# Eleven load buffers, an earlier second load, shared fills and straight programs in a fused matmul, mask and softmax

## The chip, the cores and the metric

One core of one Trainium2 chip. The metric is device time in microseconds (us) of one execution, lower is better. A kernel was run several times; a "profile" is one execution with the hardware profiler on. On one core, an execution is labelled slow when it took over 1.5% more than the fastest of the same kernel in the same set of runs.

## The reference

```
batch, m, k, n = 16, 512, 512, 512        # all float32
y = scale * (x @ weight)                  # scale = 0.125
y = where(mask == 1, y, -1e9)             # mask: strictly below the diagonal
out = softmax(y, axis=-1)
```

x is 16.8 MB, weight 1 MB, the result 16.8 MB.

## The kernel before

The work is cut into 16 units: four batches times a quarter (128) of the rows, 1 MB in, 1 MB out. A unit with quarter q needs only (q + 1) x 128 columns, the rest of its output is zero and is filled once in each output buffer. Per unit: VectorE casts x to bf16, TensorE transposes it, VectorE and ScalarE each move half of the transposes out of PSUM, TensorE multiplies with W and adds the mask on the diagonal block by one more matmul, ScalarE takes the exponential with its row sums, VectorE normalises. SyncE issues every transfer, in this order:

```python
BUFS = 8
load(0)
nc.sync.dma_start(w_f32, weight...)
load_mask(3)
load(1); load(2); load(3); load_mask(2); load(4); load_mask(1)
load(5); load_mask(0); load(6); load(7)
nc.sync.wait_ge(s_fill, 1)
for u in range(U):                                  # U = 16
    b = u % BUFS
    nc.sync.wait_ge(s_norm, u + 1)                  # unit u is normalised
    nc.sync.dma_start(out_r[...], ots[b]...)        # store u
    if u + BUFS < U:
        load(u + BUFS)                              # only now: the ninth load follows the first store
```

TensorE's start (cut):

```python
spin(WARM)                        # 12 idle matmuls, to have the clock up (1.0 from 6.3 us on in the first profile)
transpose(0, k)
spin(8)
tensor.wait_ge(s_spread, 1)
tensor.wait_ge(s_wbf, 2)          # both halves of W are cast
for j in range(1, Q):
    transpose(j, k)               # unit 1 is transposed ...
    multiply(j - 1, k)            # ... ahead of the product of unit 0
```

VectorE and ScalarE run loops of two passes over the eight buffers, with branches at their ends. GpSimd fills six parts of output buffers and prepares the mask.

The softmax here doesn't subtract the row's maximum and nothing guards it: scores larger than these inputs give would overflow.

## Time and profile before

| | first profile of the kernel before |
|---|---|
| timed runs | 94.63 us median (94.43 to 94.68) |
| the profiled execution itself | 93.16 us, span 91.0 us |
| traffic | 34.90 MB, mean 384 GB/s |
| busiest compute engine | PE 67% of the span |
| time from issue to landing, loads / stores | 14.0 / 12.3 us (medians) |

The lines themselves stand in the prediction. To read them: a row of slices gives the busy share of 40 equal parts of the span in tenths; GB/s is what the 16 DMA engines moved in each; a stretch's line ends in granted TensorE clock, DMA share and GB/s; a timeline line starts with start and duration in us.

### The profile page before, as it was taken

What the parts mean: (1) busy time and instruction counts of PE and PEld (TensorE: products, weight loads), DVE (VectorE), ACT (ScalarE), POOL (GpSimd) and SP (SyncE); (2) the same over time, 40 slices, a digit from 0 to 9 for tenths busy, and PEclk for the clock granted to TensorE, in tenths of its full rate; (3) what the DMA queues carried; (4) which work ended last, traced back from release to release, by engine and by line L of the source; (5) the groups of instructions that cost most, each with busy time, mean ns of one, the idle gap of its engine ahead of it and who ended that gap; (6) DMA issues with size and microseconds to landing.
All of it is one profiled execution on the core that took longest, in us unless ns stands there. A gap on an engine that the chain in (4) does not pass through costs nothing.

```text
span 91.0 us, 1718 instructions
## 1 busy us (share of the span) xinstructions
PE 60.8 (67%) x592; PEld 42.4 (47%) x596; DVE 56.6 (62%) x70; ACT 52.9 (58%) x149; POOL 11.1 (12%) x18
## 2 busy tenths in 40 slices
PE   0894904999986699998399999817999594000000
PEld 0333404466865547697364778806465483000000
DVE  1005555809999992999997499969281999600000
ACT  0700941778978468897978889734788495000000
POOL 3770596101700000000000000000000000000000
PEclk9999999999999999999999999999999999655555
DMA  0999999999999999999999999999999999999940
GB/s 7 328 396 384 412 418 405 398 375 424 426 421 328 263 378 418 429 425 407 443 411 439 414 421 439 407 439 414 425 436 411 443 414 439 421 421 432 418 202 11
DMA packets 5331, 34.90 MB, mean 384 GB/s; under 512 B 592, under 2 KB 1104, under 8 KB 1104
## 3 DMA queue, kind: packets, MB, share of 16 engines
q1 hardware_dynamic: 5328, 34.87, 94.3%
q8 instruction: 1, 0.02, 0.1%
q14 instruction: 2, 0.02, 0.1%
HBM read 18.09 MB, written 16.78 MB: 383 GB/s over the span
## 4 chain that ended last, share of the span: by engine, by line
DMA 31%; DVE 29%; PE 12%; issue 9%; SPq 4%; DVEq 0%
DMA xf<-in_x_dram 31%; DVE xb L214 13%; DVE ot L227 10%; PE py L332 7%; DVE xt L218 5%; PE pt L317 4%; SPq L123 2%; DVE rinv L225 1%; SPq L119 1%; SPq L142 1%; SPq L126 1%; PE py L339 0%; DVE ot L233 0%; DVEq L213 0%; DVEq L224 0%
## 5 line engine op out<-in xcount | busy, mean ns | idle before, releaser
L332 PE MATMUL py<-w_bf,xt 128*128 128x384 bf16 (+3 forms) x252 | 39.2, 298 | 0.2
L298 ACT ACTIVATE ot<-py 128x512 f32<-128x512 f32 (+3 forms) x64 | 27.8, 439 | 6.0 <-PE py L339 4.4
L214 DVE CAST xb<-xf 128x2048 bf16<-128x2048 f32 x16 | 20.6, 1288 | 11.4 <-DMA xf<-in_x_dram 11.4
L317 PE MATMUL pt<-ident_bf,xb 128*128 128x128 bf16 x256 | 17.2, 220 | 12.4 <-DVE xb L214 12.3
L332 PEld LDWEIGHTS py<-w_bf,xt 128*128 128x128 bf16 x256 | 21.0, 98 | 8.7 <-issue 0.2
L274 ACT COPY xt<-pt 128x1024 bf16<-128x1024 bf16 x16 | 16.2, 1010 | 15.3 <-PE pt L317 15.3
L227 DVE TENSOR_TENSOR ot<-ot,rinv 128x2048 f32<-128x2048 f32 (+3 forms) x16 | 23.9, 1492 | 0.5
L317 PEld LDWEIGHTS pt<-ident_bf,xb 128*128 128x128 bf16 x256 | 15.0, 114 | 15.7 <-DVE xb L214 15.2
L218 DVE COPY xt<-pt 128x1024 bf16<-128x1024 bf16 x16 | 11.0, 686 | 8.4 <-PE pt L317 8.3
L339 PE MATMUL py<-diag_bf,spread 128*128 128x128 bf16 x64 | 14.0, 219 | 0.0
L298 ACT ACTIVATION_READ_ACCUMULATOR ot<-py 128x1 f32 x64 | 12.7, 199 | 0.0
L352 PE MATMUL idle<-zeros 128*128 128x512 bf16 x20 | 6.5, 488 | 2.6 <-DVE zeros L238 2.6
L339 PEld LDWEIGHTS py<-diag_bf,spread 128*128 128x128 bf16 x64 | 6.3, 98 | 3.1
L162 POOL MEMSET ot<- 128x512 f32 (+2 forms) x6 | 6.0, 1008 | 1.5 <-issue 1.1
L352 PEld LDWEIGHTS idle<-zeros 128*128 128x128 bf16 x20 | 2.3, 119 | 5.8 <-issue 5.0
L187 POOL TENSOR_SCALAR diag_bf<-diag_f 128x128 bf16<-128x128 f32 x4 | 2.5, 634 | 11.3 <-DMA diag_f<-in_mask_dram 11.3
L225 DVE RECIPROCAL rinv<-rsum 128x4 f32<-128x4 f32 x16 | 2.7, 170 | 0.0
L274 ACT ACT_TABLE_LOAD x2 | 2.6, 1283 | 0.0
L280 ACT ACT_TABLE_LOAD x1 | 1.3, 1283 | 2.2 <-issue 2.2
L165 POOL MEMSET ot<- 4x384 f32 x2 | 1.8, 890 | 0.1
L238 DVE MEMSET zeros<- 128x256 uint32 x1 | 0.3, 272 | 1.6 <-SPq L64 1.6
L286 ACT CAST w_bf<-w_f 128x1024 bf16<-128x1024 f32 x1 | 1.0, 1049 | 0.0
(9 smaller groups left out, 2.9 us busy)
## 6 DMA issues: line engine op xcount, KB each, us to landing
xf<-in_x_dram SPq DMA_DIRECT2D x16, 1024.0 KB, 14.0
out_dram<-ot SPq DMA_DIRECT2D x16, 1024.0 KB, 12.3
w_f<-in_weight_dram SPq DMA_DIRECT2D x1, 1024.0 KB, 7.9
diag_f<-in_mask_dram SPq DMA_DIRECT2D x4, 64.0 KB, 12.2
```

The costliest lines, as they stand in the source:

```text
L162: pool_step(nc.gpsimd.memset(ots[b][:, :, NC:], 0.0))
L187: nc.gpsimd.tensor_scalar(out=diag_bf[:, q], in0=diag_f32[:, q], scalar1=-MASK_NEG, scalar2=MASK_NEG, op0=ALU.mult, op1=ALU.add,)
L214: vector.tensor_copy(xb, xfs[u % BUFS]).then_inc(s_cast[u % Q], 1)
L218: vector.tensor_copy(xts[u % 2][:, 2:4], pts[1]).then_inc(s_evv[u % Q], 1)
L225: vector.reciprocal(rinvs[b], rsums[b]).then_inc(s_inv[b], 1)
L227: mul = vector.tensor_tensor(out=ot, in0=ot, in1=rinvs[b].unsqueeze(2).to_broadcast([P, T, NC]), op=ALU.mult)
L274: scalar.copy(xts[u % 2][:, 0:2], pts[0]).then_inc(s_eva[u % Q], 1)
L298: scalar.activation(out=ots[j][:, t, :NC], in_=pys[t][:, :NC], func=AF.Exp, bias=0.0, scale=float(scale), accum_out=rsums[j][:, t : t + 1] ...
L317: last = tensor.transpose(pts[kt // 2][:, kt % 2, t], xb[:, t].rearrange("p (k kt) -> p kt k", kt=KT)[:, kt], ident_bf,)
L332: tensor.matmul(pys[t][:, :NC], lhsT=xts[j % 2][:, kt, t], rhs=w_bf[:, kt, :NC], start=(kt == 0), stop=(kt == KT - 1),)
L339: tensor.matmul(pys[t][:, q * P : NC], lhsT=spread[:, t], rhs=diag_bf[:, q], start=False, stop=True, skip_group_check=True,).then_inc(s_py ...
L352: tensor.matmul(idle, lhsT=zeros[:, :P], rhs=zeros, start=True, stop=True)
```

## The change

Its intent: let the transfers never wait for compute. Three more loads are issued before the first store; the second load goes ahead of W, so that TensorE can transpose unit 1 while W arrives; fills leave GpSimd in part; loops become straight programs.

```diff
-BUFS = 8
+X_BUFS = 11
+OUT_BUFS = 8
 ...
     load(0)
+    load(1)
     nc.sync.dma_start(w_f32, weight...)
     load_mask(3)
-    load(1)
     load(2)
-    load(3) ... load(7)                         # with the masks between
-    nc.sync.wait_ge(s_fill, 1)
+    for u in range(3, X_BUFS):
+        load(u)
+        if u < Q + 2:
+            load_mask(Q + 1 - u)
+    nc.sync.wait_ge(s_fill, 3)
 ...
-        if u + BUFS < U:
-            load(u + BUFS)
+        if u + X_BUFS < U:
+            load(u + X_BUFS)
 ...  # VectorE: for u in range(U), no loop registers; W is cast after unit 1's cast and eviction
 ...  # ScalarE: three fills ahead of its first eviction; unit 1 is evicted ahead of W's cast
 ...  # TensorE:
                 spin(8)
-                tensor.wait_ge(s_spread, 1)
-                tensor.wait_ge(s_wbf, 2)
 ...
                     transpose(j, k)
+                    if j == 1:
+                        with tensor.If(k < 2):
+                            spin(4)
+                            tensor.wait_ge(s_spread, 1)
+                            tensor.wait_ge(s_wbf, 2)
                     multiply(j - 1, k)
```

More of the change, by code (lines that the diff above doesn't have):

```diff
@@ L57 @@
     U = B
-    PASSES = U // BUFS
     x_r = x.rearrange("(c e) (q p t) k -> c q p e (t k)", e=E, q=Q, t=T)
@@ L87 @@
     zeros = sbuf("zeros", [P, N], BF16)
-    ots = [sbuf(f"ot{i}", [P, T, N], FP32) for i in range(BUFS)]
-    xfs = [sbuf(f"xf{i}", [P, T, K], FP32) for i in range(BUFS)]
+    ots = [sbuf(f"ot{i}", [P, T, N], FP32) for i in range(OUT_BUFS)]
+    xfs = [sbuf(f"xf{i}", [P, T, K], FP32) for i in range(X_BUFS)]
     xb = sbuf("xb", [P, T, K], BF16)
     xts = [sbuf(f"xt{i}", [P, KT, T, P], BF16) for i in range(2)]
-    rsums = [sbuf(f"rsum{i}", [P, T], FP32) for i in range(BUFS)]
-    rinvs = [sbuf(f"rinv{i}", [P, T], FP32) for i in range(BUFS)]
+    rsums = [sbuf(f"rsum{i}", [P, T], FP32) for i in range(OUT_BUFS)]
+    rinvs = [sbuf(f"rinv{i}", [P, T], FP32) for i in range(OUT_BUFS)]
     pts = [psum(f"pt{i}", [P, 2, T, P], BF16) for i in range(2)]
@@ L98 @@
     s_issued = sem("s_issued")
-    s_x = sem("s_x", BUFS)
-    s_o = sem("s_o", BUFS)
+    s_x = sem("s_x", X_BUFS)
+    s_o = sem("s_o", OUT_BUFS)
     s_mask = sem("s_mask", Q)
@@ L108, with nth, right @@
     s_exp = sem("s_exp", Q, T)
-    s_inv, s_mul = sem("s_inv", BUFS), sem("s_mul", BUFS)
-    s_norm = sem("s_norm")
+    s_own, s_norm = sem("s_own"), sem("s_norm")
     def quarter(u):
         return Q - 1 - u % Q
+    def nth(u):
+        return u // Q + 1
+    def right(b):
+        return ots[b][:, :, (quarter(b) + 1) * P :]
     def load(u):
-        b = u % BUFS
+        b = u % X_BUFS
         nc.sync.dma_start(xfs[b].rearrange("p t k -> p (t k)"), x_r[u // Q, quarter(u)]).then_inc(s_x[b], 16)
@@ L125 @@
     load(0)
+    load(1)
     nc.sync.dma_start(w_f32, weight.rearrange("(p kt) n -> p kt n", kt=KT)).then_inc(s_w, 16)
     load_mask(3)
-    load(1)
     load(2)
-    load(3)
-    load_mask(2)
-    load(4)
-    load_mask(1)
-    load(5)
-    load_mask(0)
-    load(6)
-    load(7)
-    nc.sync.wait_ge(s_fill, 1)
+    for u in range(3, X_BUFS):
[3 more added lines that the diff above has]
+    nc.sync.wait_ge(s_fill, 3)
     for u in range(U):
-        b = u % BUFS
+        b = u % OUT_BUFS
         nc.sync.wait_ge(s_norm, u + 1)
         nc.sync.dma_start(out_r[u // Q, quarter(u)], ots[b].rearrange("p t n -> p (t n)")).then_inc(
-            s_o[b] if u + BUFS < U else s_end, 16
+            s_o[b] if u + OUT_BUFS < U else s_end, 16
         )
-        if u + BUFS < U:
-            load(u + BUFS)
+        if u + X_BUFS < U:
+            load(u + X_BUFS)
     nc.sync.sem_inc(s_issued, 1)
@@ L157, in pool_step @@
         nc.gpsimd.wait_ge(s_pool, steps)
-    def fill(b):
-        NC = (quarter(b) + 1) * P
-        if NC < N:
-            pool_step(nc.gpsimd.memset(ots[b][:, :, NC:], 0.0))
-        if NC == P:
-            pool_step(nc.gpsimd.memset(ots[b][0:E, 0, NC:], 1.0 / N))
     pool_step(nc.gpsimd.memset(ident_bf, 0.0))
@@ L178 @@
         nc.gpsimd.sem_inc(s, 1)
-    for s in s_o:
-        nc.gpsimd.sem_inc(s, 16)
-    for b in range(BUFS // 2):
-        fill(b)
+    for b in range(1, Q):
+        pool_step(nc.gpsimd.memset(right(b), 0.0))
+    nc.gpsimd.sem_inc(s_fill, 1)
+    nc.gpsimd.wait_ge(s_fill, 2)
+    for b in range(Q - 1, OUT_BUFS, Q):
+        pool_step(nc.gpsimd.memset(right(b)[0:E, 0], 1.0 / N))
+    nc.gpsimd.sem_inc(s_fill, 1)
     for j in range(Q):
@@ L185 @@
         nc.gpsimd.wait_ge(s_mask[q], 16)
-        pool_step(
-            nc.gpsimd.tensor_scalar(
-                out=diag_bf[:, q],
-                in0=diag_f32[:, q],
-                scalar1=-MASK_NEG,
-                scalar2=MASK_NEG,
-                op0=ALU.mult,
-                op1=ALU.add,
-            )
-        )
-        nc.gpsimd.sem_inc(s_diag, 1)
-        if j == 0:
-            for b in range(BUFS // 2, BUFS):
-                fill(b)
-            nc.gpsimd.sem_inc(s_fill, 1)
+        nc.gpsimd.tensor_scalar(
+            out=diag_bf[:, q],
+            in0=diag_f32[:, q],
+            scalar1=-MASK_NEG,
+            scalar2=MASK_NEG,
+            op0=ALU.mult,
+            op1=ALU.add,
+        ).then_inc(s_diag, 1)
     nc.gpsimd.wait_ge(s_issued, 1)
@@ L209, with cast, evict_v, normalise @@
     vector = nc.vector
-    def cast(u, k, m):
-        vector.wait_ge(s_x[u % BUFS], m * 16)
-        vector.tensor_copy(xb, xfs[u % BUFS]).then_inc(s_cast[u % Q], 1)
-    def evict_v(u, k):
-        vector.wait_ge(s_ptb[u % Q], k)
+    def cast(u):
+        b = u % X_BUFS
+        vector.wait_ge(s_x[b], 16 * (u // X_BUFS + 1))
+        vector.tensor_copy(xb, xfs[b]).then_inc(s_cast[u % Q], 1)
+    def evict_v(u):
+        vector.wait_ge(s_ptb[u % Q], nth(u))
         vector.tensor_copy(xts[u % 2][:, 2:4], pts[1]).then_inc(s_evv[u % Q], 1)
-    def normalise(u, k, m):
-        b, j = u % BUFS, u % Q
+    def normalise(u):
+        b, j = u % OUT_BUFS, u % Q
         NC = (quarter(u) + 1) * P
         ot = ots[b][:, :, :NC]
-        vector.wait_ge(s_exp[j][T - 1], k + 1 if j >= Q - 2 else k)
-        vector.reciprocal(rinvs[b], rsums[b]).then_inc(s_inv[b], 1)
-        vector.wait_ge(s_inv[b], m)
+        vector.wait_ge(s_exp[j][T - 1], nth(u) + (j >= Q - 2))
+        vector.reciprocal(rinvs[b], rsums[b]).then_inc(s_own, 1)
+        vector.wait_ge(s_own, 2 * u + 1)
         mul = vector.tensor_tensor(
@@ L230, in normalise @@
         if NC == P:
-            mul.then_inc(s_mul[b], 1)
-            vector.wait_ge(s_mul[b], m)
+            mul.then_inc(s_own, 1)
+            vector.wait_ge(s_own, 2 * u + 2)
             vector.memset(ots[b][0:E, 0, :NC], 1.0 / N).then_inc(s_norm, 1)
@@ L235, in normalise @@
             mul.then_inc(s_norm, 1)
+            vector.sem_inc(s_own, 1)
     vector.addr_align(LINE, max_nops=0)
-    vector.memset(zeros, 0.0).then_inc(s_zero, 1)
-    cast(0, 1, 1)
-    evict_v(0, 1)
-    vector.wait_ge(s_w, 16)
-    vector.tensor_copy(w_bf[:, 0:2], w_f32[:, 0:2]).then_inc(s_wbf, 1)
-    cast(1, 1, 1)
-    evict_v(1, 1)
-    cast(2, 1, 1)
-    with vector.Fori(1, PASSES + 1) as m:
-        ks = [m * 2 + (i - 1) for i in range(3)]
-        ks.append(None)
-        for j in range(BUFS):
-            def ahead():
-                evict_v(j + 2, ks[(j + 2) // Q])
-                if j + 3 < BUFS:
-                    cast(j + 3, None, m)
-            def far():
-                if j + 2 >= BUFS:
-                    evict_v(j + 2, ks[(j + 2) // Q])
-                cast(j + 3, None, m + 1)
-            if j + 2 < BUFS:
-                ahead()
-            if j + 3 >= BUFS:
-                with vector.If(m < PASSES):
-                    far()
-            normalise(j, ks[j // Q], m)
+    with vector.Fori(0, 2) as n, vector.If(n > 0):
+        vector.memset(zeros, 0.0).then_inc(s_zero, 1)
+        cast(0)
+        evict_v(0)
+        cast(1)
+        evict_v(1)
+        vector.wait_ge(s_w, 16)
+        vector.tensor_copy(w_bf[:, 0:2], w_f32[:, 0:2]).then_inc(s_wbf, 1)
+        cast(2)
+        for u in range(U):
+            if u + 2 < U:
+                evict_v(u + 2)
+            if u + 3 < U:
+                cast(u + 3)
+            normalise(u)
@@ L270, with evict_s @@
     scalar = nc.scalar
-    def evict_s(u, k):
-        scalar.wait_ge(s_pta[u % Q], k)
+    def evict_s(u):
+        scalar.wait_ge(s_pta[u % Q], nth(u))
         scalar.copy(xts[u % 2][:, 0:2], pts[0]).then_inc(s_eva[u % Q], 1)
     scalar.addr_align(LINE, max_nops=0)
-    with scalar.Fori(0, 2) as n, scalar.If(n > 0), scalar.Fori(1, PASSES + 1) as m:
-        with scalar.If(m < 2):
-            scalar.wait_ge(s_ident, 1)
-            scalar.copy(
-                spread.rearrange("k t (p e) -> k t p e", e=E),
-                ident_bf.rearrange("k (p t) -> k t p", t=T).unsqueeze(3).to_broadcast([P, T, P // T, E]),
-            ).then_inc(s_spread, 1)
-            evict_s(0, 1)
-            scalar.wait_ge(s_w, 16)
-            scalar.copy(w_bf[:, 2:4], w_f32[:, 2:4]).then_inc(s_wbf, 1)
-        ks = [m * 2 + (i - 1) for i in range(3)]
-        for j in range(BUFS):
-            if j + 1 < BUFS:
-                evict_s(j + 1, ks[(j + 1) // Q])
-            else:
-                with scalar.If(m < PASSES):
-                    evict_s(j + 1, ks[(j + 1) // Q])
-            NC = (quarter(j) + 1) * P
-            scalar.wait_ge(s_o[j], m * 16)
+    with scalar.Fori(0, 2) as n, scalar.If(n > 0):
+        scalar.wait_ge(s_ident, 1)
+        scalar.copy(
+            spread.rearrange("k t (p e) -> k t p e", e=E),
+            ident_bf.rearrange("k (p t) -> k t p", t=T).unsqueeze(3).to_broadcast([P, T, P // T, E]),
+        ).then_inc(s_spread, 1)
+        scalar.wait_ge(s_zero, 1)
+        for b in range(Q + 1, OUT_BUFS):
+            NF = N - (quarter(b) + 1) * P
+            fill = scalar.copy(right(b), zeros[:, :NF].unsqueeze(1).to_broadcast([P, T, NF]))
+        fill.then_inc(s_fill, 1)
+        evict_s(0)
+        evict_s(1)
+        scalar.wait_ge(s_w, 16)
+        scalar.copy(w_bf[:, 2:4], w_f32[:, 2:4]).then_inc(s_wbf, 1)
+        for u in range(U):
+            b, j = u % OUT_BUFS, u % Q
+            NC = (quarter(u) + 1) * P
+            if 0 < u < U - 1:
+                evict_s(u + 1)
+            if u >= OUT_BUFS:
+                scalar.wait_ge(s_o[b], 16 * (u // OUT_BUFS))
@@ L296 @@
             for t in range(T):
-                scalar.wait_ge(s_py[j % Q][t], ks[j // Q])
+                scalar.wait_ge(s_py[j][t], nth(u))
                 scalar.activation(
-                    out=ots[j][:, t, :NC],
+                    out=ots[b][:, t, :NC],
                     in_=pys[t][:, :NC],
@@ L303 @@
                     scale=float(scale),
-                    accum_out=rsums[j][:, t : t + 1],
-                ).then_inc(s_exp[j % Q][t], 1)
+                    accum_out=rsums[b][:, t : t + 1],
+                ).then_inc(s_exp[j][t], 1)
     tensor = nc.tensor
@@ L376 @@
     with tc.tile_critical(no_gpsimd_drain=True):
-        nc.sync.wait_ge(s_end, 16 * BUFS)
+        nc.sync.wait_ge(s_end, 16 * OUT_BUFS)
         nc.sync.sem_clear(s_end)
```

## The prediction

> **What bounds the kernel now.** I read the page's slices first, because they show whether one resource is busy from end to end.
>
> ```profile
> DVE  1005555809999992999997499969281999600000
> ACT  0700941778978468897978889734788495000000
> DMA  0999999999999999999999999999999999999940
> GB/s 7 328 396 384 412 418 405 398 375 424 426 421 328 263 378 418 429 425 407 443 411 439 414 421 439 407 439 414 425 436 411 443 414 439 421 421 432 418 202 11
> ```
>
> A slice is 2.275 us. The DMA row is at 9 from the second slice to the second-last but one; no compute row is, and all of them are empty in the last 5 to 6 slices while transfers go on. So the 16 DMA engines bound the kernel: 34.90 MB in a span of 91.0 us. The rate has three defects: a start (328 to 384), a dip to 263 around slice 13, and a tail. I put numbers on them with busy time by stretch (us, busy times of the engines, granted clock, DMA share, GB/s last).
>
> ```profile
> 10.00:20.00 10.00, 6.30 (x51) 3.62 (x51) 4.97 (x5) 5.74 (x11) 5.14 (x6) 1.00 1.01 401
> 20.00:28.00 8.00, 7.62 (x91) 6.19 (x89) 7.37 (x8) 7.04 (x21) 1.93 (x2) 1.00 1.01 422
> 28.00:33.00 5.00, 3.54 (x41) 2.47 (x39) 4.97 (x7) 3.02 (x12) 0.00 (x0) 1.00 0.99 283
> 34.00:80.00 46.00, 36.18 (x384) 26.85 (x383) 36.41 (x48) 33.56 (x103) 0.00 (x0) 0.98 1.01 425
> 80.00:85.00 5.00, 0.00 (x0) 0.00 (x0) 0.00 (x0) 0.00 (x0) 0.00 (x0) 0.50 1.03 434
> ```
>
> Steady traffic of loads and stores mixed runs at 425, stores alone at 434, loads alone at 422 once the mask loads are through. The dip, 28 to 33 us, moves 283. It costs 5 x (1 - 283/425) = 1.67 us. Its DMA share is 0.99: the engines were **not empty** in it. The packet records of the trace say the same: an 8 KB packet takes 309 ns nearly everywhere, but in these 5 us many take 400 to 660 ns and five take 1.3 to 1.95 us.
>
> What the dip coincides with is in the timeline of the queue that issues:
>
> ```profile
> 24.89 0.61 SPq L142 DMA_DIRECT2D out_dram<-ot  x1
> 25.54 0.60 SPq L119 DMA_DIRECT2D xf<-in_x_dram  x1
> 28.44 0.60 SPq L142 DMA_DIRECT2D out_dram<-ot  x1
> 29.08 0.84 SPq L119 DMA_DIRECT2D xf<-in_x_dram  x1
> 31.52 0.60 SPq L142 DMA_DIRECT2D out_dram<-ot  x1
> 32.16 1.03 SPq L119 DMA_DIRECT2D xf<-in_x_dram  x1
> ```
>
> The first store is issued at 24.89 and the ninth load at 25.54, when the eight first loads are still draining (the eighth was issued by 10.6 and lands 17.2 us after its issue, near 27.2). So the dip begins just as the engines pass from loads to the first store, with two transfers queued and the next pair coming at 28.44. That makes two readings possible: a **thin queue**, or a **first store that is slow by itself**. This is the fork of the whole prediction.
>
> Last, the chain that ended last:
>
> ```profile
> 4.37 8.09 DMA xf<-in_x_dram
> 12.47 0.02 issue
> 12.49 2.33 DVE xb L214
> 14.82 0.05 issue
> 14.87 1.08 PE pt L317 x16
> 15.95 0.05 issue
> 16.00 0.81 PE py L332 x3
> ```
>
> Compute of the first unit (4 batches x 128 rows; there are 16) begins only at 16.00, since TensorE transposes unit 1 ahead of the first product, unit 1 lands at 12.47 behind W, and its cast takes 2.33 us. This start is late, but it is on the path that sets the end only in so far as it delays transfers.
>
> [...] the store issued at 24.89 lands 5.9 us later (30.8), after the eighth load. So in the changed kernel the first store stands behind eleven loads. [...] the cast that ran from 12.49 beside a GpSimd fill took 2.32 us, the median of that row is 1217 ns. [...] the register steps on VectorE's sequencer in the chain are 0.04 to 0.05 us each.
>
> **The change part by part.**
>
> *Second load ahead of W.* Each MB takes about 2.6 us at the early rate of 401. The first load lands at 7.1 (0.96 + 6.1) as before; the second now near 9.7 in place of 12.47; W near 12.2 in place of 9.6. The cast of unit 1 can end near 10.9, its transposes near 12.1, and then W is the last to come: 12.2 + 1.05 (ScalarE's cast of its half) = 13.25. The first product starts near 13.3 in place of 16.0: 2.7 us earlier. The first store, 8.9 us after it (24.89 - 16.00), comes near 22.2. No byte of traffic is removed, and the transfers of these first 13 us are merely permuted: 0 us at the end by itself.
>
> *Fills shared.* Three memsets of GpSimd (3.31 us from 10.43) become three copies on ScalarE. As estimates they cost about as much (512, 1024 and 1536 elements a row, some 3.5 us), from 4 to 7.6 us, ahead of the first eviction at 9.1: hidden. The cast loses its 1.1 us of blocking. Off the DMA path: 0 us.
>
> *Straight programs.* Register steps and branches go: some 0.05 to 0.2 us a unit on VectorE. Where VectorE is the pace, four stores come in 15.33 us (40.16 to 55.49), 3.83 a unit, against 2 MB a unit at 425, 4.9 us. VectorE is not the pace of the transfers: 0 us.
>
> *Eleven load buffers.* Before the first store there are now 11 loads, W and the masks: 11 x 1.049 + 1.049 + 0.26 = 12.85 MB. At 402 GB/s, from 2.4 us, that lasts to about 34.3. By then (first store 22.2, then about 3 to 4 us each, as before) four stores and four loads are queued. The queue is never thin: 8 MB in place of 2. The last load moves up, from 70.35 to about 60. After it there are only stores; the DMA engines reach store k (from the sixth on) at 59 + 2.45 (k - 5), hence the last at 83.5, and compute has it ready by about 77 (3.83 x 15 + 22.2 less the uneven last unit), so no gap opens there. Output buffers stay at eight: the thirteenth unit's exponential (near 60) needs the fifth store (near 58); close, but with slack of 4 us at the end.
>
> *Sum.* Transfers after the change: 2.4 + 12.85 MB/402 + 22.0 MB/425 = 2.4 + 32.0 + 51.8 = 86.2, plus the tail. The same sum for before, 9.7 MB/402 + 25.2 MB/425 = 24.1 + 59.3, plus 2.4 and the 1.67 of the dip, gives 87.5. The tail and the end are equal. The longer stretch of loads at 402 is an artefact of the masks in it, which do not grow; with 422 for the three added loads the difference is the dip alone, **1.67 us if it goes altogether, 0 if it stays**.
>
> **The rivals.** *A: thin queue.* With 8 MB queued the dip goes: 94.63 - 1.67 = 93.0; since the five engines that were held for 1 to 1.6 us longer may be those that finish last (the slice rates fall 418, 202, 11), perhaps up to 1 us more: 92.0. For it: the dip sits exactly where the queue is thinnest, and the rate is full from 34 on, with the queue deeper. Against it: the first store and ninth load were queued over 2 us before their turn and the share is 0.99. *B: the first stores are slow whenever they come,* [...]. Then the dip moves to 34 us and the time stays at 94.3 to 94.6. For it: the slow packets are those of the first store itself. Against it: stores alone at 80 to 85 us run at 434. *C: compute or the eight output buffers become the bound* after the loads have run ahead: stores late, a new gap near 60 to 75 us, 95 or more. For it: the fifth store comes close to the exponential that needs it; against it: 4 to 6 us of slack for the last stores.
>
> **Range and chances.** I give A a little over half[...], and B a little under half: 0.53 x 92.7 + 0.44 x 94.4 + 0.03 x 95.5 = 93.5. The runs of before spread by 0.25 us. Two per cent faster means below 92.74, which needs the whole dip and some of the tail: about 0.25. Over 2% slower needs C at its worst: 0.02. The range that should hold it 8 times in 10 is 92.0 to 94.7.
>
> **What would show it.** First product near 13.3 and first store issued near 22: the compute part. Rate in 28 to 33 at 420 and no dip near 34 to 39: A. A dip of the same depth, moved to about 34 to 39, with DMA share near 1: B. Last load landing near 60. Waits of ScalarE for a store, or a DMA share below 0.9 between 55 and 80: C. The prediction is wrong if the start of the transfers itself moves, or if the engines that finish last are not relieved although the dip goes.

## The result

The changed kernel took **91.14 us** (median, 91.02 to 91.44, 4 runs), the kernel before 94.66 us (94.43 to 96.43, 4 runs). The ratio of the fast runs is 0.9641, 95% interval 0.9607 to 0.9674; a ratio here is the mean time of one kernel's fast runs over that of the other's in the same rounds, so not quite the ratio of the medians. The kernel is 3.6% faster. The prediction said 93.5, with 92.0 to 94.7: too little gain, and the time lies outside of the range.

The profile of the changed kernel (91.09 us, span 89.3) answers to the lines above. First the slices:

```profile
DVE  0105545329999983999997499999669994000000
ACT  0199444688977478897558889746798960000000
DMA  0999999999999999999999999999999999999940
GB/s 7 305 404 407 417 409 421 368 380 415 424 418 429 433 426 418 426 422 429 415 426 426 422 426 429 426 418 433 426 422 426 426 429 418 429 433 426 426 187 11
```

The dip of the thirteenth and fourteenth slices is gone and none has come elsewhere: from the tenth slice to the 38th the rate stays between 415 and 433. By stretch, same columns as before:

```profile
28.00:33.00 5.00, 3.77 (x32) 2.36 (x33) 4.93 (x8) 2.73 (x8) 0.00 (x0) 1.00 1.01 426
...
40.00:80.00 40.00, 28.77 (x315) 21.57 (x312) 30.87 (x41) 25.60 (x86) 0.00 (x0) 0.97 1.01 426
80.00:85.00 5.00, 0.00 (x0) 0.00 (x0) 0.00 (x0) 0.00 (x0) 0.00 (x0) 0.50 1.02 429
```

283 became 426 where the dip was; the steady stretch stayed what it was (425, now 426), and stores alone ran at 429 for 434. The queue that issues:

```profile
23.91 0.61 SPq L145 DMA_DIRECT2D out_dram<-ot  x1
24.57 0.60 SPq L126 DMA_DIRECT2D xf<-in_x_dram  x1
27.46 0.60 SPq L145 DMA_DIRECT2D out_dram<-ot  x1
28.10 0.60 SPq L126 DMA_DIRECT2D xf<-in_x_dram  x1
```

The first store is issued only 1 us earlier than before, but its turn on the DMA engines comes near 34 (33.95) instead of 27 (26.54), behind eleven loads. Last, the chain at the start:

```profile
10.52 1.14 DVE xb L206
11.66 0.05 issue
11.71 0.65 PE pt L299 x8
12.36 0.02 issue
12.38 1.01 ACT xt L253
13.39 0.95 ACT w_bf L270
14.35 0.47 issue
14.82 1.02 PE py L314 x4
```

The first product starts at 14.82 instead of 16.00; ScalarE first evicts unit 1 (1.01) and then casts W, which I had not put in the sum.

So at this point the mechanism looks like my rival A. What does not fit is the size: the spans of the two profiles differ by 1.7 us, which is the dip, and the times by 3.5.

### The profile page after: what moved, and what is told of

The parts are those of the page before. It is cut to its first block, busy times and chain, and to the rows that moved or that the text cites. A ratio compares the mean times of both kernels' runs of the same rounds, so it can differ in the third digit from the quotient of the medians.

```text
span 89.3 us, 1698 instructions
## 1 busy us (share of the span) xinstructions
PE 61.1 (68%) x599; PEld 42.7 (48%) x600; DVE 55.3 (62%) x70; ACT 52.7 (59%) x150; POOL 5.9 (7%) x15
## 4 chain that ended last, share of the span: by engine, by line
DVE 27%; PE 26%; issue 20%; DMA 7%; ACT 2%; SPq 0%; DVEq 0%
PE py L314 16%; DVE xb L206 15%; PE pt L299 10%; DVE xt L210 9%; DMA xf<-in_x_dram 7%; DVE rinv L217 1%; ACT xt L253 1%; DVE ot L219 1%; ACT w_bf L270 1%; PE py L321 1%; DVE ot L225 0%; DVEq L231 0%; SPq L397 0%; SPq L64 0%
## 5 line engine op out<-in xcount | busy, mean ns | idle before, releaser
L314 PE MATMUL py<-w_bf,xt 128*128 128x512 bf16 (+3 forms) x256 | 40.0, 299 | 1.2 <-ACT w_bf L270 1.2
L206 DVE CAST xb<-xf 128x2048 bf16<-128x2048 f32 x16 | 19.5, 1218 | 5.8 <-DMA xf<-in_x_dram 5.8
L265 ACT CAST ot<-zeros 128x512 f32<-128x512 bf16 (+2 forms) x3 | 2.9, 1040 | 0.0
L175 POOL MEMSET ot<- 128x512 f32 (+2 forms) x3 | 2.9, 951 | 0.6 <-issue 0.5
L185 POOL TENSOR_SCALAR diag_bf<-diag_f 128x128 bf16<-128x128 f32 x4 | 1.5, 375 | 12.6 <-DMA diag_f<-in_mask_dram 12.6
L180 POOL MEMSET ot<- 4x384 f32 x2 | 0.8, 408 | 3.9 <-ACT ot L265 3.9
```

Of the source, the lines that this page charges most:

```text
L175: pool_step(nc.gpsimd.memset(right(b), 0.0))
L206: vector.tensor_copy(xb, xfs[b]).then_inc(s_cast[u % Q], 1)
L265: fill = scalar.copy(right(b), zeros[:, :NF].unsqueeze(1).to_broadcast([P, T, NF]))
L314: tensor.matmul(pys[t][:, :NC], lhsT=xts[j % 2][:, kt, t], rhs=w_bf[:, kt, :NC], start=(kt == 0), stop=(kt == KT - 1),)
```

## The experiments

Five sets of two to four kernels, each set on one chip together with runs of the kernel before. Since the label "fast" in a set depends on how lucky the fastest run of the kernel before was (92.23 in the first set), most verdicts against it read "unclear"; I give medians and ranges of all runs. Each set ran on another chip, and the median of the kernel before lies between 94.31 and 95.19 in them, so a difference between two sets is rougher than one within a set.

**1. The kernel before once more** (no edit).

> The kernel before, unchanged, run as if it were the change, so that every run's span is listed and another execution is profiled. Theory 1 (my base was a lucky execution): the profiled execution that I predicted from took 93.16 us with a span of 91.0, 1.5 us less than the timed runs (94.63); then the runs here should have spans of about 92.5 and a profile whose dip between 28 and 33 us, or whose tail, costs some 1.5 us more than in the first one. Rival (the gain lies outside the span, in the launch): spans stay near 91.0 while the times are 94.6. Ratio to before 1.00.

Measured: 94.79 us (91.65 to 95.54, 4 runs) and 95.19 (92.23 to 96.46, 7 runs) for the same kernel. The kernel before is not one number: it spreads by 4 us, while the changed one spreads by 0.4. Of its 45 recorded executions four took 91.65 to 92.71 us, less than my first profile; none of them was profiled, so what made them fast stays open. The profiled execution took 95.54 with a span of 93.4, so the missing time is inside the span, as theory 1 says.

**2. Straight programs alone**: the kernel before with VectorE and ScalarE unrolled as in the change.

```diff
-    with vector.Fori(1, PASSES + 1) as m: ...
+    for u in range(U):
+        if u + 2 < U: evict_v(u + 2)
+        if u + 3 < U: cast(u + 3)
+        normalise(u)
```

> The kernel before with one part of the change alone: straight programs on VectorE and ScalarE; eight load buffers, W first, GpSimd fills. If straight programs carry nothing: ratio 1.00 to before, and the same mixture of fast and slow executions (92 to 96). Rival (branches and register steps were on the path of the first stores): first store about 0.5 us or more earlier and 1% less time.

Measured: 95.65 us (95.25 to 97.08) beside 94.76 (93.64 to 95.61) for the kernel before; ratio 1.0135 (1.0009 to 1.026). Straight programs by themselves bring nothing; if anything they lose 1.4%, which no run explains (the recorded verdict is unclear). Their profile (95.77 us) shows where the kernel with eight buffers and W first loses more than in my first profile. TensorE at the start, the idle time before an instruction in brackets:

```profile
10.73 1.24 PE L336 MATMUL idle<-zeros 128*128 128x512 bf16 x5
15.62 1.08 PE L301 MATMUL pt<-ident_bf,xb 128*128 128x128 bf16 x16 [3.64 <-DVE xb L217]
```

and the stretches of the same execution (granted clock, DMA share, GB/s last):

```profile
15.00:20.00 5.00, 4.32 (x26) 2.30 (x28) 2.38 (x3) 1.70 (x3) 1.21 (x2) 0.67 1.02 419
26.00:28.00 2.00, 2.00 (x28) 1.86 (x27) 2.00 (x3) 2.00 (x7) 0.00 (x0) 1.00 0.50 209
28.00:33.00 5.00, 3.21 (x50) 2.78 (x49) 4.93 (x7) 3.17 (x15) 0.00 (x0) 1.00 0.91 315
33.00:40.00 7.00, 6.95 (x61) 4.42 (x61) 5.28 (x8) 5.51 (x13) 0.00 (x0) 1.00 1.00 364
```

While it waits for unit 1 behind W, TensorE stands still for 3.64 us. After that its granted clock is 0.5 for 3.41 us (16.73 to 20.14 in the trace's clock records), a mean of 0.67 over this stretch. The first products come slower (four matmuls of 128x512 take 1.91 us instead of 1.03), the first store is issued at 27.32 instead of 24.89 (0.75 of these 2.4 us were lost before the clock fell, since unit 1's transposes start at 15.62 instead of 14.87), and now the queue does run out: DMA share 0.50 between 26 and 28. At 425 GB/s the lost time is 2 x (1 - 209/425) + 5 x (1 - 315/425) + 7 x (1 - 364/425) = 3.3 us, against 1.67 in my first profile. The profile of experiment 1 has the same picture (clock 0.66 between 15 and 20, first store at 27.07, 209 GB/s between 26 and 28).

Waits and clocks side by side, for the profiles with eight buffers or with W first, and for nine buffers: the longest wait of TensorE in its timeline from 9 to 20 us, and the granted clock:

| profile | longest wait, us | granted clock |
|---|---|---|
| before once more (1) | 3.69 | 0.66 between 15 and 20 |
| straight programs alone (2) | 3.64 | 0.67 between 15 and 20 |
| before, first profile | 3.64 | 1.00 between 10 and 20 |
| W ahead, eleven buffers (7) | 2.62 | 0.92 between 10 and 15, 0.74 between 15 and 20 |
| changed with eight buffers (5) | 1.99 | 0.68 between 10 and 15 |
| nine buffers (6) | 1.77 | 1.00 between 10 and 20 |
| changed with eight buffers, delayed (9) | 1.73 | 1.00 between 10 and 20 |
| order alone (4) | 1.52 | 1.00 between 10 and 20 |
| before, kept warm (3) | 1.06 | 1.00 between 10 and 20 |

After a wait of 3.64 to 3.69 us in the kernel before and this variant, the clock fell in two of three profiles. My first profile was the one in which it did not. It also fell in two profiles whose longest wait was shorter, 2.62 and 1.99 us. So the length of the wait alone does not tell whether the clock falls; what does was not shown.

**3. The kernel before, kept warm**: 12 more idle matmuls fill that wait (1.06 us of it is left), all else as before.

```diff
-                spin(8)
+                spin(20)
```

> The kernel before with 12 more idle matmuls (about 2.8 us) in the wait of TensorE between about 11.2 and 14.9 us, so that it does not stand still there; nothing else changes. In two profiles of this wait at 3.64 to 3.69 us the granted clock then fell to 0.5 for 3.4 us, in one it did not. Theory (the lowered clock delays the first store by some 2 us, the queue runs out, and this is what made my base 1.5 us too fast): the clock stays at 1 until the end of the matmuls, the first store is issued near 25 in every execution, and the times fall to 92 to 93.2 with little spread; ratio 0.97 to 0.985. Rival (the clock has nothing to do with the time): 94.7, ratio 1.00.

Measured: **93.22 us** (92.91 to 93.28) beside 94.97 (92.62 to 95.70). The spread is gone and the median is the time of my lucky profile, 93.16. The ratio of the fast runs is 0.999 (0.983 to 1.0153, unclear), since only the undisturbed runs of the kernel before count as fast: against those, keeping warm changes nothing, which is what the theory says. In its profile the dip stays, at full clock:

```profile
15.00:20.00 5.00, 4.76 (x39) 2.92 (x41) 1.96 (x3) 3.09 (x8) 0.79 (x2) 1.00 0.99 383
...
28.00:33.00 5.00, 3.54 (x43) 2.60 (x42) 4.97 (x7) 3.03 (x11) 0.00 (x0) 1.00 1.01 292
```

So the 3.5 us are two things: about 1.5 us (94.7 to 93.2) for the lowered clock, 2.1 (93.2 to 91.1) for the dip and what hangs on it. These differences are taken across sets; within this set the changed kernel with its fills on GpSimd (experiment 10, 91.20) is 2.0 us below the kept-warm one. That the clock accounts for the 1.5 us rests on three profiles of that start and on this run: the other executions of the kernel before were not profiled.

**4. Order alone**: the kernel before with the second load ahead of W and the waits moved as in the change; loops, fills and eight buffers kept.

```diff
     load(0)
+    load(1)
     nc.sync.dma_start(w_f32, weight...)
     load_mask(3)
-    load(1)
```

> The kernel before with the other part alone: second load ahead of W, the cast of W and the wait for it moved behind the transposes of unit 1; loops, fills and eight load buffers as before. Theory (slack): the first store is issued about 1 us earlier than in the kernel before at the same granted clock, so the dip shrinks: 92 to 93 where TensorE has its full clock between 10 and 20 us, 93.7 to 94.5 where it has not. Rival (order is worth 0 with eight buffers too): 94.7.

Measured: **92.14 us** (91.97 to 92.24) beside 94.76 (93.64 to 95.61); ratio of the fast runs 0.978 (0.970 to 0.987). The recorded verdict is unclear, since the interval spans the line of 2%, but it excludes 1: this goes against my step that the order is worth 0. TensorE's longest wait at the start shrinks to 1.5 us, its clock stays up there (1.00 between 10 and 20), and the first store is issued at 24.24. Most of the dip is gone too:

```profile
28.00:33.00 5.00, 3.59 (x33) 2.15 (x31) 4.93 (x8) 2.86 (x10) 0.00 (x0) 1.00 1.01 405
```

**5. Eight load buffers in the changed kernel** (`X_BUFS = 8`).

> The changed kernel with eight load buffers in place of eleven; all else as in the change. Theory A (thin queue at the first store): the loads last to about 27 us, the dip is back at its old place and depth (280 GB/s over 5 us) and the time is 94 to 94.7. Rival (order, straight programs and fills carry part of the 3.5 us): 92.5 to 93.5, with a dip of half the size. Rival B2 (the dip depends on something else than buffers): no dip, 91.2.

Measured: 92.21 us (91.46 to 93.75), verdict unclear. None of my ranges holds it; the rival's, 92.5 to 93.5, comes nearest. All else of the change leaves eight buffers within 1.1 us of eleven, as the order alone does. The profile fell on the slowest of its four runs; in it the clock had fallen after all (0.68 between 10 and 15), the first store was issued at 25.85 and 28 to 33 ran at 338.

**6. Nine load buffers** (`X_BUFS = 9`).

> The changed kernel with nine load buffers. Loads last to about 29.5 us, the first store is issued near 24, so it waits 5.5 us in the queue in place of 3 (eight) or 10 (eleven). Theory A with a threshold in time queued: most of the dip is gone, 91.5 to 92.5. If the dip scales with the buffers, a third of the gain is lost for every buffer: 93.4.

Measured: 91.84 us (90.67 to 92.00). In the profile no dip is left: 428 between 28 and 33. One buffer more is nearly enough when the clock is up (1.00 between 10 and 20); it does not scale with the buffers.

**7. W ahead of the second load, eleven buffers.**

> The changed kernel with W and the first mask ahead of the second load again, as before the change; eleven buffers. By my prediction's part on the order this is worth 0 us at the end: 91.1 to 91.4, with the first product near 14 to 15 us and the first store issued about 1.5 to 2.5 us later than in the change, still some 8 us ahead of its turn. Rival: the order carries part of the gain, 92 or more.

Measured: 91.43 us (90.60 to 91.61). Here, in the very execution profiled (91.39 us), the clock *had* fallen (0.74 between 15 and 20) and the first store came at 26.89, 3 us later than in the change; yet 28 to 33 ran at 423:

```profile
26.89 0.61 SPq L145 DMA_DIRECT2D out_dram<-ot  x1
```

```profile
28.00:33.00 5.00, 3.20 (x53) 2.83 (x51) 4.93 (x7) 2.88 (x14) 0.00 (x0) 1.00 1.01 423
```

With eleven buffers the order is worth 0 to 0.3 us. With eight (experiment 4) it is worth 2.6 against the median of the kernel before and 2.0 against the mean of its fast runs, 94.1.

**8. and 9. The first product delayed by 24 more idle matmuls**, with eleven and with eight load buffers.

```diff
-                            spin(4)
+                            spin(28)
```

> The changed kernel with 24 more idle matmuls (5.7 us) on TensorE ahead of the first product, of which about 1.2 us fall into a wait that is there anyway: the first store is issued near 28.4 in place of 23.9. Its turn on the engines is near 34 with eleven buffers. Theory (eleven buffers are worth the slack between the first store and the end of the loads): no change, 91.0 to 91.6. Rival (compute at the start is on the path): 4.5 us more, 95.7.

> The same delay with eight load buffers, all else as in the change. The loads end near 27 and the first store is issued near 28.4: the queue is empty for 2 to 3 us and the first stores are slow after it. Theory: 95 to 97, with a rate near 0 in some slice about 27 to 30. If buffers had nothing to do with it: 92.2 as with eight buffers and no delay.

Measured: **91.03 us** (90.87 to 91.06) with eleven, **95.15** (94.83 to 95.35) with eight. The first store was issued at 27.48 and 27.95. The same delay costs nothing with eleven buffers and 2.9 us with eight (95.15 - 92.21, across two sets), where the queue runs dry:

```profile
26.00:28.00 2.00, 2.00 (x29) 1.83 (x27) 2.00 (x2) 1.88 (x6) 0.00 (x0) 1.00 0.34 143
28.00:33.00 5.00, 3.47 (x50) 2.98 (x47) 4.96 (x6) 3.78 (x17) 0.00 (x0) 1.00 0.79 264
```

**10. All fills on GpSimd again**, in the changed kernel.

> The changed kernel with all fills on GpSimd as before the change. Expected by every theory: 91.0 to 91.6, since the fills lie beside the loads; a cast of VectorE beside a fill may take 2 us in place of 1.2, which delays the first store by at most 1 us of the 10 that it has.

Measured: 91.20 us (91.18 to 91.25), first store at 24.02. One cast took 2.31 us against a median of 1.22; in the first profile it was a cast beside a fill that took 2.32. Where the fills run is worth nothing here.

**11. and 12. What makes the dip where the queue is not empty?** In the kept-warm kernel nothing is missing (DMA share 1.01) and yet the rate is low (292). Two holds in the changed kernel tell a late issue from a shallow queue:

```diff
         nc.sync.wait_ge(s_norm, u + 1)
+        if u == 0: nc.sync.wait_ge(s_x[9], 16)     # 11: the first store held
+        if u == 1: nc.sync.wait_ge(s_x[10], 16)    # 12: the second store held
```

> The changed kernel, eleven buffers, but the first store is held until the tenth load has landed (about 31.8 us); after it the next stores and loads, which are ready, follow at once, 0.6 us each. So the first store has only about 2 us between its issue and its turn on the engines (near 34), while five or six transfers soon stand behind it. If it is the short time between issue and turn that makes the first store's packets slow: slow packets (over 400 ns) between 33 and 37, 0.8 to 1.6 us lost, 92 to 92.8. If it is the small number of transfers queued: no dip, 91.2 to 91.6.

> The changed kernel, eleven buffers; the first store and the twelfth load are issued near 24 as in the change, 10 us ahead of their turn, but the second store is held until the eleventh load has landed (near 36). So the queue behind the loads is only 2 MB deep, as in the kernel before, with a long time between issue and turn. If a shallow queue makes packets slow: dip between 34 and 39 as deep as before, 92.5 to 93. If the short time between issue and turn does: the first store and the twelfth load run at 309 ns, 91.2 to 91.6, with at most a little lost at the second store near 39.

Measured: 93.67 us (93.35 to 94.08) for the first store held, **91.72** (91.51 to 91.95) for the second. In 11 the tenth load landed later than I had thought, the store was issued at 33.86, and the queue did run empty for a moment (DMA share 0.71, 295 GB/s between 33 and 36), after which the rate was low with the engines busy (share 1.03, 320 between 36 and 40); so it shows that lateness costs 2.5 us even with eleven buffers, but not how early is early enough. In 12 only one store and one load stood behind the loads, as in the kernel before, but issued 10 us ahead; the rate stayed at 423 between 33 and 40 (its time is 0.1 us above the range that I expected):

```profile
24.33 0.61 SPq L147 DMA_DIRECT2D out_dram<-ot  x1
24.99 0.60 SPq L126 DMA_DIRECT2D xf<-in_x_dram  x1
36.45 0.59 SPq L147 DMA_DIRECT2D out_dram<-ot  x1
```

```profile
33.00:40.00 7.00, 7.00 (x73) 5.22 (x71) 5.28 (x7) 6.16 (x18) 0.00 (x0) 1.00 1.01 423
```

**A shallow queue alone does not make the dip.**

**13. and 14. Eleven buffers, and only the lead of the first store changed** (44 and 52 idle matmuls instead of 4). The lead is the time from the issue of the first store to the moment when the first DMA engine has finished the loads ahead of it; that moment I took from the trace's packet records (each transfer ends with a 4-byte packet on each engine: 592 in the first profile, 16 for each of 37 transfers): 33.96 and 33.89 us here. In the first profile the transfers land in the order of their issue, the eighth load at 28.18 and the first store at 30.74.

> The changed kernel with 40 more idle matmuls ahead of the first product: the first store is issued near 31.0, about 3 us ahead of the first engine's turn (near 34.0). If the lead between issue and turn decides and some 2.5 us are enough: no dip, 91.0 to 91.5.

> The changed kernel with 48 more idle matmuls ahead of the first product: the first store is issued near 32.7, about 1.3 us ahead of the first engine's turn (near 34.0), as in the kernel before, but with eleven load buffers. If the lead decides: the dip is back, now between 34 and 39 us, some 1.3 to 1.7 us are lost, 92.3 to 93. If eight buffers as such brought the dip: no dip, 91.0 to 91.5.

Measured: 91.67 us (91.39 to 91.98) for the longer lead, **93.12** (92.93 to 93.46) for the shorter. First the longer lead: the issue of the first store, and the stretches:

```profile
31.01 0.61 SPq L145 DMA_DIRECT2D out_dram<-ot  x1
```

```profile
36.00:40.00 4.00, 3.67 (x31) 2.26 (x32) 3.93 (x7) 2.39 (x5) 0.00 (x0) 1.00 1.01 420
```

Then the shorter one:

```profile
32.67 0.61 SPq L145 DMA_DIRECT2D out_dram<-ot  x1
```

```profile
36.00:40.00 4.00, 2.59 (x33) 1.87 (x31) 3.97 (x7) 2.11 (x10) 0.00 (x0) 1.00 1.01 295
```

The dip is back with eleven buffers, moved to the new end of the loads, at DMA share 1.01, and costs 1.45 us between two kernels that differ in 1.66 us of issue time. With the others:

| kernel | first store issued | first engine free | lead | lost around it | median |
|---|---|---|---|---|---|
| delayed, eight buffers (8) | 27.95 | 26.55 | -1.4 | 4.0 | 95.15 |
| straight programs alone (8) | 27.32 | 26.70 | -0.6 | 3.3 us | 95.65 |
| before once more (8) | 27.07 | 26.52 | -0.55 | 3.2 | 95.54 (that execution) |
| first store held (11) | 33.86 | 33.96 | 0.1 | 1.9 | 93.67 |
| changed with eight buffers (8) | 25.85 | 26.75 | 0.9 | 1.9 | 93.75 (that execution) |
| lead cut short (11) | 32.67 | 33.89 | 1.2 | 1.4 | 93.12 |
| before, kept warm (8) | 25.21 | 26.59 | 1.4 | 1.6 | 93.22 |
| before, first profile (8) | 24.89 | 26.54 | 1.65 | 1.7 | 93.16 (that execution) |
| order alone (8) | 24.24 | 26.45 | 2.2 | 0.4 | 92.14 |
| lead kept (11) | 31.01 | 33.96 | 2.95 | 0 | 91.67 |
| nine buffers | 24.02 | 29.02 | 5.0 | 0 | 91.84 |
| changed (11) | 23.91 | 33.95 | 10.0 | 0 | 91.14 |

"Lost" is stretch length times (1 - rate/425), summed over the stretches near the first store. The lead divides them, whatever the number of buffers: nothing is lost from some 3 us of lead, 0.4 us at 2.2, between 1.4 and 1.9 from 1.65 down to 0.1 (in no order among these), and 3.2 or more where the store is issued after its turn.

The longer-lead kernel has a second loss, which is another lesson: its compute is 7 us behind, so its last stores come late, and between 74 and 80 us only 273 GB/s move, 2.1 us lost. (The shorter lead has it too, with 280, so it isn't the difference between the two.) Its time grows by 0.5 only. By the packet records the engines of the changed kernel end between 85.5 and 87.9 us, those of this one all between 88.15 and 88.31. The first engine ends 2.65 us later, the last only 0.4 us: by these ends, as my estimate, most of the lost rate fell on engines that would otherwise have been done early. It was not shown engine by engine.

**15. and 16. What lies outside of the span.** In the profiled executions, time minus span was 2.14 to 2.20 us in the kernel before and its variants (2, 3, 4), 1.75 to 1.85 in all that derive from the changed one.

```diff
+    s_extra = sem("s_extra", 15)                               # 15
+    for _ in range(8): nc.gpsimd.sem_inc(s_extra, 16)          # 16, one semaphore
```

> The changed kernel with 15 semaphores more, which nothing uses; the kernel before and both of its one-part variants (straight programs alone, order alone) have as many as this. In all four of those the time is 2.15 to 2.2 us over the span of the profile, in all ten kernels derived from the changed one it is 1.75 to 1.85. If the number of semaphores costs the 0.4 us outside of the span: time minus span near 2.2, median near 91.5. If not: near 1.8 and 91.1.

> The changed kernel with eight semaphore increments on GpSimd near its start, as the kernel before has for its output buffers (on one added semaphore that nothing waits for). The rival cause of the same 0.4 us. If these cost it: time minus span near 2.2, median near 91.5. If not: near 1.8 and 91.1.

Measured: 91.11 us in both (90.87 to 91.36, 90.71 to 91.36), time minus span 1.79 and 1.80. Neither is the cause. These 0.4 us stay open.

## Why the prediction was wrong

**The base was wrong; this is the step that failed.** Rival A reads "94.63 - 1.67 = 93.0". The 1.67 us came from a profile that took 93.16 us, and I took it off a median of 94.63. The 1.5 us between those two stood in the table of times and I gave them no cause. By experiments 1 to 3 they were the lowered clock, which that one profile did not have. From its own 93.16, the sum gives 91.5, and with the "up to 1 us more" for the engines that finish last, 90.5 to 91.5: the measured 91.14 lies in it. That is partly luck: the relief of the last engines did not show in the span, and 0.4 us of the gain lie outside of it, of which the prediction has nothing. With the right base, the same weights would have given 93.5 - 1.5 = 92.0. What the kept-warm kernel (93.22) and the changed one (91.14) show as the worth of the dip is 2.1 us: 1.7 in the span and 0.4 outside of it, still unexplained.

**"Merely permuted: 0 us at the end by itself" was wrong for the order.** I saw the late start on the chain and said that it matters only in so far as it delays transfers. It does delay them, in two of the three profiles with that start: 3.64 to 3.69 us of idle TensorE, clock 0.5, first store over 2 us later (27.07 and 27.32 instead of 24.89), an empty queue (DMA share 0.50 between 26 and 28). Alone, the order is worth 2.6 us of median (94.76 to 92.14); with eleven buffers it is worth next to nothing (91.43 and 91.14). The two parts cover the same loss, so their gains do not add: 2.6 alone for the order, 3.8 for all the rest without it (95.19 to 91.43 in that set), 3.5 together.

**The fork was put right and weighed too evenly.** Queue and first store were the two readings. Truth lies between: the first store was slow where it was issued 1.2 to 1.65 us before its turn (283 to 295 GB/s at a DMA share of 0.99 to 1.01), and at full rate where it was issued 2.95 us before it or more (418 to 431 by stretch). What I held against A, that the first store and ninth load "were queued over 2 us before their turn", was measured to the start of the dip near 28; the first engine was free at 26.54, a lead of 1.65. Rival B is refuted by the changed kernel itself, whose first stores run at 426 (33 to 36 us). Why a short lead slows so many packets, no run shows.

Three readings of the lines were off. The 17.2 us to landing is the median of two loads, the seventh and the eighth; the eighth alone landed at 28.2, not near 27.2. And "the slow packets are those of the first store itself" holds for a part only: of the 173 packets of 8 KB that started between 28 and 33 us, 74 took over 400 ns, and 23 of these started after 31 us, when the first store had landed (30.8). Six, not five, took 1.28 to 1.95 us.

**Compute start: direction right, size off.** First product 14.82 instead of 13.3, first store 23.91 instead of 22.2: I left ScalarE's eviction of unit 1, 1.01 of the 1.5 us, out of the order on that engine, and it costs nothing at the end. **Fills**: 2.94 us on ScalarE for an estimate of 3.5, worth 0 as said. **Straight programs**: no gain, as said. **Last load** lands near 61 (predicted about 60). **Rival C** did not come: no wait of ScalarE for a store is in the list of waits, and 40 to 80 runs at 426.

## What to carry to other kernels

When a transfer-bound kernel turns from loads to stores, look at the time from the issue of the first store to its turn on the DMA engines; here 2.95 us made it free, while 1.65 us cost 1.7. Buffers that lengthen the run of loads buy exactly that slack: with eleven, a first store 3.6 us later (experiment 8) still gave 91.03, and one 3 us later at a lowered clock (0.74, experiment 7) 91.43. Before taking a difference read in a profile off a median, ask whether the profiled execution took the median's time, and if it did not, why: a spread between executions is part of what a change can remove. And parts of a change that cover the same loss do not add, so measure each alone and together.

## Also measured

- The lead and the packets: in the first profile, with a lead of 1.65 us, 74 of the 173 packets of 8 KB that started between 28 and 33 us took over 400 ns, where the median of all is 309, although the engines were not empty (283 GB/s at a DMA share of 0.99). In the changed kernel, with a lead of 10 us, it was one of 261 between 34 and 39 us.
- The start of the first load: in the first profile the instruction that issues it ran from 0.96 to 1.62 and its first packet started at 2.46, 1.5 us after the start of the instruction and 0.8 after its end.
- The ends of the engines: they lay 2.4 us apart in the changed kernel (85.5 to 87.9), and 0.16 us apart in experiment 13 (88.15 to 88.31), whose rate was low shortly before (273 GB/s between 74 and 80), with 2.1 us of lost rate and 0.5 us of lost time.
